# A decoder trunk on one core: the second attention map is added unscaled, weight sums work in half pieces, stores are issued later

## The chip, the cores and the metric

The program runs on one core of one Trainium2 chip. Its five engines work side by side, each from a queue of its own: TensorE (PE) multiplies matrices, VectorE (DVE) and ScalarE (ACT) work elementwise, GpSimd (POOL) does some elementwise work and here issues most stores, SyncE (SP) issues the loads. The metric is the device time of one execution in microseconds (us), as the median of three.

## The reference, cut to what matters

One layer over 2048 prompt tokens and eight single-token samples: pooling mixer and differential attention, cross-attention, a gated MLP, norms between. The change touches two parts. The differential attention of a head has two score maps:

```python
s = einsum('bqhcd,bkhcd->bhcqk', q, k) * 64 ** -0.5   # c = 0, 1
a = softmax(s + alibi_bias, causal)                   # each map on its own
w = a[:, :, 0] - lam * a[:, :, 1]
o = einsum('bhqk,bkhe->bqhe', w, v)
o = rmsnorm(o, subln_g, 1e-5) * (1 - lam_0)           # over the 128 channels of a head
```

The MLP multiplies the normed tokens by `w_up` (1024 x 5632) in float32.

## The kernel before

**Numbers.** Every product of the projections is made of three matmuls over a high and a low part of each operand, the high part by an ACT copy, the low part by a DVE subtraction (`split`, L93, and the weights' stages at L307 and L310).

**Stages.** Tokens go in four chunks of 512. Within the profiled span: the projections of chunks 0 and 1 (to about 300 us), the projections of chunks 2 and 3 woven with the attention of chunks 0 and 1 (to about 640 us), the attention of chunks 2 and 3 woven with output projection, norms and first cross-attention work (to about 1110 us), the rest of the cross-attention and the samples' attention (to about 1680 us), and the MLP (to the end).

**Attention.** A `Unit` (L1088) is 128 query rows of one head against up to 2048 keys, in halves of 1024 columns. PE makes the scores of both maps (L1111). DVE adds the position bias and finds the row's extreme (L1122), ACT takes the exponential in place with its row sum `l` (L1129). `combine` (L1133) makes `rc` = (1/l0, -lam/l1) on DVE (L1138, L1139), and POOL scales the second map T1 by rc[1] (L1141). `combine2` (L1143) on DVE makes T0 = T0 * rc[0] + T1 (L1146). PE turns T0 (`wT`, L1152), ACT copies it out (L1154), PE multiplies by V into `O` (L1163). After four units `att_post1` (L1186) norms `O` into `on`, and `att_post2` turns and stores it.

**Weight sums.** `sums_items` (L1510) builds, for each of 22 blocks of `w_up`, four sums and differences of quarter blocks that the MLP uses later: two loads of 512 KB on SP's queue (L1519), four DVE instructions of 128x512 (L1528 to L1532), two splits, four stores of 512 KB on POOL's queue (L1541) into `s_d`.

**Order.** The work is a list of items; `weave` spreads a second list through a first by each item's costs. `later` puts off a function until a clock, summed up from the costs of PE's items, has gone on by so much, and `due` runs what is due. Each engine then gets its instructions in an order that a scheduler of the framework sets, which can put rows of other units between two that the code issues together.

**Buffers.** Large tiles (1024 columns and more) share one ring of 41 buffers (`H`), smaller ones a ring of 6 (`St`); a new tile takes the buffer of the one 41 or 6 requests earlier, and waits until that is free, which for a stored tile is when its store has landed. SP and POOL issue in order.

Of the kernel before, what the change touches and what calls it, by code (L numbers as in the profile page):

```python
# [11 lines left out]
F32 = mybir.dt.float32  # L12
F32R = mybir.dt.float32r
# [35 lines left out]
def tile_trunk_step(ctx: ExitStack, tc: tile.TileContext, a, o):  # L49
# [12 lines left out]
    def H(name, dt=F32):  # L62
        return hp.tile([P, HT], dt, tag="H", name=name)

    def St(name, dt=F32):
        return sp.tile([P, SW], dt, tag="S", name=name)
# [4 lines left out]
    def Tn(name):  # L71
        return tp.tile([P, 8], F32, tag="t", name=name)
# [7 lines left out]
    def v3(t, k, n=None):  # L80
        n = n if n is not None else 1024 // k
        return t[:, : k * n].rearrange("p (k n) -> p k n", k=k)
# [4 lines left out]
    def f(ap):  # L87
        return ap.bitcast(F32)
# [267 lines left out]
    def item(specs, fn, cost=0.0, lat=0.0):  # L356


        return (specs, fn, cost, max(lat, cost, 0.3))
# [412 lines left out]
    def v_proj(vt, chunks):  # L772
        st = {}

        def fn(c, t2):
            def run(ws):
# [12 lines left out]
                if t2 == 2:  # L789
# [4 lines left out]
                    for hh in range(2):  # L794
# [3 lines left out]
                vv = St("vv")  # L798
                S.copy(vv[:, :512], ps)
                t0 = c * CH + 2 * t2 * P  # L800
                ST.dma_start(o["v_p"][0, 0, t0:t0 + 256, 2 * vt:2 * vt + 2, :].rearrange("(t p) h e -> p t (h e)", p=P),
                             v3(vv, 2, 256))
                j0 = (c % 2) * 4 + 2 * t2
                for hh in range(2):
                    ST.dma_start(v_d[c // 2][2 * vt + hh][:, j0:j0 + 2, :], v3(vv, 2, 256)[:, :, hh * P:(hh + 1) * P])
            return run

        specs = [cols256("w_in", 1536 + vt * 256, 0), cols256("w_in", 1536 + vt * 256, 1)]
# [255 lines left out]

    def att_load(h, nhf, old):
        def fn(_):
            K = [[None, None] for _ in range(2)]
            Vt = [None, None]
            for hf in range(nhf):
                for c in range(2):  # L1070
                    K[c][hf] = H("K", F32R)
                    SY.dma_start(f(K[c][hf][:, :1024]), k_d[hf][h][c])
                Vt[hf] = H("V")
                SY.dma_start(v3(Vt[hf], 8), v_d[hf][h])
            att[h, nhf] = (K, Vt)
        return fn
# [11 lines left out]
    class Unit:  # L1088
# [42 lines left out]
            return item([], fn, self.halves[hf][1] / 512 * 0.43)  # L1131

        def combine(self, _):  # L1133
            l, T1 = self.l, self.T[1]
            if len(self.halves) == 2:
                V.tensor_tensor(l[:, 0:2], l[:, 0:2], l[:, 2:4], ALU.add)
            self.rc = rc = Tn("rc")
            V.reciprocal(rc[:, 0:2], l[:, 0:2])  # L1138
            V.tensor_tensor(rc[:, 0:2], rc[:, 0:2], lamv, ALU.mult)  # L1139
            for hf, (k0, m) in enumerate(self.halves):  # L1140
                G.tensor_scalar(T1[hf][:, :m], T1[hf][:, :m], rc[:, 1:2], 1.0, ALU.mult, ALU.mult)  # L1141

        def combine2(self, _):  # L1143
            for hf, (k0, m) in enumerate(self.halves):
                T0, T1 = self.T[0][hf], self.T[1][hf]
                V.scalar_tensor_tensor(T0[:, :m], T0[:, :m], self.rc[:, 0:1], T1[:, :m], ALU.mult, ALU.add)  # L1146

        def turn(self, g):
            js = range(4 * g, min(4 * g + 4, self.i + 1))
# [36 lines left out]
    def att_post1(qc, h):  # L1186
        O = att["O", qc, h]
        sq = St("osq")
        S.activation(sq[:, :512], O, AF.Square)
        ss = Tn("oss")  # L1190
        V.tensor_reduce(ss[:, 0:4].rearrange("p (a o) -> p a o", o=1), v3(sq, 4, P), AX.X, ALU.add)
        r = rstd(ss[:, 0:4], P, 4, 1.0 / P, SUB_EPS)
        on = St("on")
        V.tensor_tensor(v3(on, 4, P), v3(O, 4, P), bc(r, [P, 4, P], 2), ALU.mult)
        att["on", qc, h] = on
# [314 lines left out]
    def sums_items(js):  # L1510


        st = {}

        def load(j):
            def fn(_):
                wa, wg = H("wa"), H("wg")
                for t, c0 in ((wa, j * P), (wg, DFF + j * P)):
                    SY.dma_start(v3(t, 8), a["w_up"][0, :, c0:c0 + P].rearrange("(k p) n -> p k n", p=P))  # L1519
                st[j] = wa, wg  # L1520
            return item([], fn, 0, 1.0)

        def add(j, i):
            def fn(_):
                wa, wg = st[j]
                a1, a2, g1, g2 = wa[:, :512], wa[:, 512:1024], wg[:, :512], wg[:, 512:1024]
                if i:
                    V.tensor_tensor(a1, g2, a1, ALU.subtract)  # L1528
                    V.tensor_tensor(a2, a2, a1, ALU.subtract)
                else:  # L1530
                    V.tensor_tensor(g2, g1, g2, ALU.add)
                    V.tensor_tensor(g1, a1, g1, ALU.subtract)  # L1532
            return item([], fn, 0, 1.0)

        def part(j, i):
            def fn(_):
                t = st[j][i]
                hi, lo = H("shi", F32R), H("slo", F32R)
                split(hi[:, :1024], lo[:, :1024], t[:, :1024])
                for z, p in enumerate((hi, lo)):  # L1540
                    ST.dma_start(s_d[j][:, i, z].rearrange("p s n -> p (s n)"), f(p[:, :1024]))  # L1541
            return item([], fn, 0, 1.0)

        out = []
        for j in js:
            out += [load(j), add(j, 0), add(j, 1), part(j, 1), part(j, 0)]
        return out

    def k4(t):
# [395 lines left out]
```

## Time and profile before

| | us |
|---|---|
| median of 3 runs (lowest, highest) | 3116.74 (3115.84, 3120.43) |
| the profiled execution's own time | 3116.27 |
| its span, first to last instruction | 3114.6 |
| PE busy in the span | 2939.9 (94%) |
| DVE busy | 2240.0 (72%) |
| ACT busy | 1351.9 (43%) |
| POOL busy | 516.2 (17%) |

The span is 1.7 us shorter than the execution's time. PE is busy for nearly all of it, and the share of PE is lowest in the first 100 us and between 300 and 1110 us. A wait is put down to the instruction whose end came last; the chain of waits follows the last instruction back to what released it, step by step.

### The profile page before, as it was taken

The page shows a single profiled execution, that of the slowest core. Times are in us where ns is not written, and L with a number is a line of the kernel's source. Part 1 is how long each engine was busy: PE and PEld are TensorE (multiplying, and loading weights), DVE is VectorE, ACT ScalarE, POOL GpSimd, SP SyncE. Part 2 cuts the span into 40 slices and gives each one's busy share as a digit, 9 for nine tenths or more (in the row PEclk, how much of TensorE's full clock was granted, in tenths as well). Part 3 has the DMA queues.
Part 4 walks back from the last instruction along what each step waited for, and adds up shares of the span by engine and source line. Part 5 has one row for each costly group of instructions (what it writes and reads, how often), then busy time and mean ns, then how long its engine had stood idle before and what let it go on. Part 6 is the DMA issues. An engine that isn't in the chain of part 4 may idle for free.

```text
span 3114.6 us, 52466 instructions
## 1 busy us (share of the span) xinstructions
PE 2939.9 (94%) x19806; PEld 2650.3 (85%) x19806; DVE 2240.0 (72%) x4032; ACT 1351.9 (43%) x2271; POOL 516.2 (17%) x961
## 2 busy tenths in 40 slices
PE   7999899889899898999989999999999999999998
PEld 6778789778788687689978899888899989999998
DVE  5734666467776668666778978888888777877777
ACT  5534445355665442334333344444444433443333
POOL 0244235312111115421000000010000010000000
PEclk9999999989999999999999999999999999999999
DMA  8777478835353357658759876687776786576762
GB/s 280 243 270 241 135 238 263 265 97 186 115 173 119 110 176 255 203 171 282 276 190 332 294 247 220 211 275 249 238 253 217 236 291 209 178 262 218 240 210 105
DMA packets 520511, 683.14 MB, mean 219 GB/s; under 512 B 27472, under 2 KB 342359, under 8 KB 520243
## 3 DMA queue, kind: packets, MB, share of 16 engines
q1 hardware_dynamic: 466525, 533.87, 52.8%
q0 software_dynamic: 39936, 135.17, 12.2%
q10 hardware_dynamic: 13798, 10.76, 1.1%
q8 instruction: 156, 2.56, 0.3%
q14 instruction: 96, 0.79, 0.1%
HBM read 549.12 MB, written 130.98 MB: 218 GB/s over the span
## 4 chain that ended last, share of the span: by engine, by line
PE 59%; DVE 8%; issue 4%; DMA 2%; ACT 2%; POOL 1%; DVEq 0%; ACTq 0%; POOLq 0%; SPq 0%
PE up L1613 15%; PE down L1729 15%; PE up L1615 7%; PE wo L483 3%; PE upB L1613 2%; PE S L99 2%; PE S L101 2%; PE S L100 2%; PE O L1163 2%; PE vo L99 1%; PE vo L100 1%; PE vo L101 1%; PE upB L1615 1%; PE sc L1111 1%; DVE T L1122 1%
## 5 line engine op out<-in xcount | busy, mean ns | idle before, releaser
L1729 PE MATMUL down<-act,whi 128*128 128x512 f32 (+1 forms) x1760 | 452.1, 351 | 3.2 <-ACT whi L307 3.1
L1613 PE MATMUL up<-xhi,shl 128*128 128x256 f32 (+1 forms) x2816 | 406.9, 285 | 7.9 <-DVE s L1618 6.3
L1613 PEld LDWEIGHTS up<-xhi,shl 128*128 128x128 f32 x2816 | 365.1, 188 | 37.9 <-DVE s L1618 13.2
L1667 ACT ACTIVATE cc<-Uf,vec 128x512 f32<-128x512 f32 (+1 forms) x176 | 143.9, 818 | 502.6 <-DVE Uf L1618 491.6
L310 DVE TENSOR_TENSOR wlo<-wraw,whi 128x1024 fp32r<-128x1024 f32 x256 | 310.2, 1220 | 38.5 <-ACT whi L307 30.2
L1729 PEld LDWEIGHTS down<-act,whi 128*128 128x128 f32 x1760 | 286.5, 189 | 36.6 <-ACT whi L307 3.5
L307 ACT CAST whi<-wraw 128x1024 fp32r<-128x1024 f32 x256 | 265.3, 1047 | 102.3 <-DMA wraw<-in_w_down_dram 29.3
L1729 PE MATMUL down<-act,wlo 128*128 128x512 f32 (+1 forms) x880 | 280.2, 350 | 0.1
L1672 POOL COPY halo<-Uf 128x2 f32<-128x2 f32 x176 | 56.7, 322 | 1275.5 <-DVE Uf L1618 1250.5
L1129 ACT ACTIVATE T<-T,mn 128x1024 f32<-128x1024 f32 (+4 forms) x192 | 171.9, 897 | 131.2 <-DVE mn L1122 120.5
L1615 PE MATMUL up<-xlo,shl 128*128 128x256 f32 (+1 forms) x1408 | 223.8, 281 | 0.0
L1111 PE MATMUL sc<-K,Q 128*128 128x512 f32 (+5 forms) x640 | 176.6, 394 | 37.8 <-DVE mn L1122 36.3
L1613 PE MATMUL up<-xhi,whl 128*128 128x256 f32 (+1 forms) x1408 | 199.3, 284 | 8.8 <-DVE whl L329 4.9
L1613 PEld LDWEIGHTS up<-xhi,whl 128*128 128x128 f32 x1408 | 183.9, 189 | 17.5 <-DVE whl L329 6.1
L1615 PEld LDWEIGHTS up<-xlo,shl 128*128 128x128 f32 x1408 | 191.3, 188 | 0.3
L1675 DVE SCALAR_TENSOR_TENSOR cc<-Uf,vec,cc 128x512 f32<-128x512 f32 x176 | 131.6, 748 | 73.6 <-ACT cc L1667 73.5
L329 DVE TENSOR_TENSOR whl<-wraw,whl 128x512 fp32r<-128x512 f32 x264 | 178.5, 683 | 0.4 <-ACT whl L327 0.4
L1733 DVE TENSOR_TENSOR xf<-xf,down 128x512 f32<-128x512 f32 (+1 forms) x240 | 134.9, 578 | 56.2 <-PE down L1729 55.0
L1729 PEld LDWEIGHTS down<-act,wlo 128*128 128x128 f32 x880 | 154.1, 188 | 22.5 <-DVE wlo L310 0.9
L1122 DVE CUSTOM_DVE_ANT_0 T<-sc,Dt 128x1024 f32<-128x1024 f32 (+7 forms) x128 | 125.8, 985 | 64.0 <-PE sc L1111 49.3
L1618 DVE TENSOR_TENSOR Uf<-up,s 128x256 f32<-128x256 f32 (+1 forms) x264 | 111.6, 423 | 83.0 <-PE up L1615 80.5
L327 ACT CAST whl<-wraw 128x512 fp32r<-128x512 f32 x264 | 155.2, 614 | 25.4 <-PE up L1615 6.4
(437 smaller groups left out, 7124.5 us busy)
## 6 DMA issues: line engine op xcount, KB each, us to landing
shl<-s_d SPq DMA_DIRECT2D x352, 512.0 KB
wraw<-in_w_up_dram SPq DMA_DIRECT2D x264, 256.0 KB
wraw<-in_w_down_dram SPq DMA_DIRECT2D x88, 512.0 KB
s_d<-shi POOLq DMA_DIRECT2D x44, 512.0 KB
s_d<-slo POOLq DMA_DIRECT2D x44, 512.0 KB
wraw<-in_w_in_dram SPq DMA_DIRECT2D x32, 512.0 KB
Q<-q_d SPq DMA_DIRECT2D x64, 256.0 KB
wraw<-in_w_out_dram SPq DMA_DIRECT2D x32, 512.0 KB
```

The source lines that it names most:

```text
L307: S.copy(self.hi[:, :1024], self.raw[:, :1024])
L310: V.tensor_tensor(self.lo[:, :1024], self.raw[:, :1024], f(self.hi[:, :1024]), ALU.subtract)
L327: S.copy(self.hl[:, :512], self.raw)
L329: V.tensor_tensor(self.hl[:, 512:1024], self.raw, f(self.hl[:, :512]), ALU.subtract)
L1111: PE.matmul(ps[:, j * 512:j * 512 + w], v3(Q[c], 2)[:, z, self.t * P:(self.t + 1) * P], K[c][hf][:, c0:c0 + w], start=z == 0, stop=z == 1)
L1122: V.tensor_tensor_reduce(out, pin, din, -SLOPE[self.h], 3.0e38 if hf == 0 else mn[:, 0:1], ALU.add, ALU.min, mn[:, hf:hf + 1])
L1129: S.activation(tg[:, :mg], tg[:, :mg], AF.Exp, bias=mn[:, last:last + 1], scale=-1.0, accum_out=self.l[:, 2 * g + c:2 * g + c + 1])
L1613: PE.matmul(out, wi[:, k, :], xh[:, k], start=k == 0 and wi is wl, stop=False)
L1615: PE.matmul(out, wh[:, k, :], xl[:, k], start=False, stop=k == 3)
L1667: S.activation(cc[:, :w], U[:, 2:2 + w], AF.Identity, bias=vc(CB + nt), scale=vc(CWT + 2 * FT + nt))
L1729: PE.matmul(out, st["w"][0][wi][:, p, n0:n0 + P], act[:, z + c0:z + c0 + n], start=st_ and p == 0, stop=en and p == g - 1)
L1733: V.tensor_tensor(xx[:, c0:c0 + n], xx[:, c0:c0 + n], out, ALU.add)
```

## The change

Four edits. **One:** T1 is no longer scaled by POOL. `combine` makes rc = (1/l0, 1/l1) and then rc[1] = l0 * (-lam) * (1/l1), and `combine2` makes T0 = T1 * rc[1] + T0, which is l0 times the old result. 1/l0 of the four units is kept in a tile `rcu` and comes in behind the values: `att_post1` multiplies the mean square twice by 1/l0 ahead of the root, and the root's reciprocal once. **Two:** the weight sums work on half pieces of a block, each in one buffer `ws`: four loads of 128 KB, four DVE instructions of 128x256, one split, two stores of 512 KB, each of them written in four runs of 256 columns per partition. The loads count 1.5, the other steps 0.5 each in the weave, 6 for a block where it was 5. **Three:** the sums' stores are an item behind the split. **Four:** the stores of V are put off by 2.6 on the clock (or until K and V are loaded), and the copy that the attention reads goes ahead of the output's.

```diff
@@ v_proj
-                ST.dma_start(o["v_p"]...)
                 j0 = (c % 2) * 4 + 2 * t2
-                for hh in range(2):
-                    ST.dma_start(v_d[c // 2][2 * vt + hh]...)
+                def store():
+                    for hh in range(2):
+                        ST.dma_start(v_d[c // 2][2 * vt + hh]...)
+                    ST.dma_start(o["v_p"]...)
+                later(2.6, store, "v")
@@ att_load
+            due("v")
@@ Unit.combine, combine2
-            self.rc = rc = Tn("rc")
-            V.reciprocal(rc[:, 0:2], l[:, 0:2])
-            V.tensor_tensor(rc[:, 0:2], rc[:, 0:2], lamv, ALU.mult)
-            for hf, (k0, m) in enumerate(self.halves):
-                G.tensor_scalar(T1[hf][:, :m], T1[hf][:, :m], rc[:, 1:2], 1.0, ALU.mult, ALU.mult)
+            if self.t == 0:
+                att["rc", self.qc, self.h] = tp.tile([P, 8], F32, tag="rcu", name="rcu", bufs=6)
+            rc = att["rc", self.qc, self.h][:, 2 * self.t:2 * self.t + 2]
+            self.rc = rc[:, 1:2]
+            V.reciprocal(rc, l[:, 0:2])
+            V.scalar_tensor_tensor(self.rc, l[:, 0:1], lamv[:, 1:2], self.rc, ALU.mult, ALU.mult)
...
-                V.scalar_tensor_tensor(T0[:, :m], T0[:, :m], self.rc[:, 0:1], T1[:, :m], ALU.mult, ALU.add)
+                V.scalar_tensor_tensor(T0[:, :m], T1[:, :m], self.rc, T0[:, :m], ALU.mult, ALU.add)
@@ att_post1
+        r0 = att["rc", qc, h][:, 0:8:2]
+        for _ in range(2):
+            V.tensor_tensor(ss[:, 0:4], ss[:, 0:4], r0, ALU.mult)
         r = rstd(ss[:, 0:4], P, 4, 1.0 / P, SUB_EPS)
+        V.tensor_tensor(r, r, r0, ALU.mult)
@@ sums_items
+        def load(j, q):
+                w = st[j, q] = H("ws")
+                for i, c0 in enumerate((j * P, DFF + j * P)):
+                    for h in range(2):
+                        r0 = h * 512 + q * 256
+                        SY.dma_start(v3(w[:, i * 512 + h * 256:i * 512 + (h + 1) * 256], 2, P),
+                                     a["w_up"][0, r0:r0 + 256, c0:c0 + P].rearrange("(k p) n -> p k n", p=P))
+            return item([], fn, 0, 1.5)
+        def add(j, q):
...
+                V.tensor_tensor(g2, g1, g2, ALU.add)        # and three more of 128x256
+        def part(j, q):
+                split(st["p"][0][:, :1024], st["p"][1][:, :1024], st.pop((j, q))[:, :1024])
+        def store(j, q):
+                for z, p in enumerate(st["p"]):
+                    ST.dma_start(s_d[j][:, :, z, :, q * 256:(q + 1) * 256], f(v3(p, 4)).rearrange("p (i s) n -> p i s n", i=2))
-            out += [load(j), add(j, 0), add(j, 1), part(j, 1), part(j, 0)]
+            for q in range(2):
+                out += [load(j, q), add(j, q), part(j, q), store(j, q)]
```

How this moves instructions is seen at three places. On DVE in the attention of chunks 2 and 3, where a unit with 1920 keys is combined beside the norm of the cross-attention's input (`h2lo`, `wlo` are splits), there stood before:

```order
L281 TENSOR_TENSOR h2lo<-x,h2hi 128x2x512
L1138 RECIPROCAL rc<-l 128x2
L1122 ISA T,mn<-sc,Dt 128x1024
L1122 ISA mn 128x1
L1139 TENSOR_TENSOR rc<-rc,lamv 128x2
L310 TENSOR_TENSOR wlo<-wraw,whi 128x1024 x2
L1146 SCALAR_TENSOR_TENSOR T<-T,rc 128x1024
L1146 SCALAR_TENSOR_TENSOR T<-T,rc 128x896
```

and near it in the change, where L1127 is the old L1122, L1146 and L1147 make the factors and L1152 is the combination:

```order
L1127 ISA T,mn<-sc,Dt,mn 128x128
L1127 ISA mn 128x1
L1146 RECIPROCAL rcu<-l 128x2
L1147 SCALAR_TENSOR_TENSOR rcu<-l,lamv,rcu 128x1
L1152 SCALAR_TENSOR_TENSOR T<-T,rcu 128x1024
L1127 ISA T,mn<-sc,Dt 128x1024
L1127 ISA mn 128x1
L310 TENSOR_TENSOR wlo<-wraw,whi 128x1024 x2
L1152 SCALAR_TENSOR_TENSOR T<-T,rcu 128x1024
```

The combination follows its factors at once; the splits that stood between them now stand behind its first half. On DVE at the end of four units (`oss` is the sum of squares, `rv` to `ry` the root), before:

```order
L187 TENSOR_SCALAR rv<-oss 128x4
L1528 TENSOR_TENSOR wa<-wg,wa 128x512
L190 TENSOR_TENSOR rt<-ry 128x4
L1529 TENSOR_TENSOR wa<-wa 128x512
L191 TENSOR_TENSOR rt<-rt,rv 128x4
L1122 ISA T,mn<-sc,Dt,mn 128x896
```

and at the same place in the change (L1200 is the new product with 1/l0, L1542 the last of the sums):

```order
L1197 TENSOR_REDUCE oss<-osq 128x4
L310 TENSOR_TENSOR wlo<-wraw,whi 128x1024 x2
L1200 TENSOR_TENSOR oss<-oss,rcu 128x4
L1141 TENSOR_TENSOR l<-l 128x2
L1542 TENSOR_TENSOR ws<-ws 128x256
L1200 TENSOR_TENSOR oss<-oss,rcu 128x4
L1146 RECIPROCAL rcu<-l 128x2
L187 TENSOR_SCALAR rv<-oss 128x4
L1147 SCALAR_TENSOR_TENSOR rcu<-l,lamv,rcu 128x1
L1152 SCALAR_TENSOR_TENSOR T<-T,rcu 128x1024
```

Two more small rows stand between the sum of squares and the root, with rows of other work between them. On POOL, where the projections of chunks 2 and 3 come to V, before:

```order
L1141 TENSOR_SCALAR T<-T,rc 128x1024
L1541 DMA s_d_156<-shi 128x1024
L1541 DMA s_d_156<-slo 128x1024
L801 DMA out_v_p_dram<-vv 128x2x256
L805 DMA v_d_0_140<-vv 128x2x128
L805 DMA v_d_1_141<-vv 128x2x128
L1541 DMA s_d_156<-shi 128x1024
L1541 DMA s_d_156<-slo 128x1024
L1141 TENSOR_SCALAR T<-T,rc 128x128
```

and in the change (L1554 are the sums' stores, L805 and L806 those of V):

```order
L1554 DMA s_d_156<-shi 256x2x256
L1554 DMA s_d_156<-slo 256x2x256
L755 COPY zsT<-kf 128x8
L744 DMA k_d_3_135<-kh 64x512 x2
L744 DMA k_d_3_135<-kl 64x512 x2
L751 DMA out_k_p_dram<-ks 128x4x128
L805 DMA v_d_0_140<-vv 128x2x128
L805 DMA v_d_1_141<-vv 128x2x128
L806 DMA out_v_p_dram<-vv 128x2x256
L1554 DMA s_d_156<-shi 256x2x256
```

POOL's queue holds stores and small copies alone there; the scalings are gone from between them.

## Rows read from the trace of the kernel before

**Rows 1.** The page: the span and the busy time of the engines.
```profile
span 3114.6 us, 52466 instructions
PE 2939.9 (94%) x19806; PEld 2650.3 (85%) x19806; DVE 2240.0 (72%) x4032; ACT 1351.9 (43%) x2271; POOL 516.2 (17%) x961
```

**Rows 2.** Stretches: length, PE, PEld, DVE, ACT, POOL busy; PE's clock, DMA, GB/s.
```profile
97.00:300.00 203.00, 197.86 (x1107) 169.25 (x1105) 113.33 (x165) 89.79 (x138) 76.19 (x135) 1.00 0.79 259
300.00:720.00 420.00, 381.37 (x2478) 342.62 (x2479) 259.68 (x545) 195.72 (x386) 131.50 (x205) 0.95 0.64 204
720.00:1110.00 390.00, 348.84 (x2342) 309.03 (x2341) 279.16 (x501) 228.74 (x441) 68.58 (x74) 0.97 0.42 137
1110.00:1684.00 574.00, 532.23 (x3354) 464.81 (x3353) 396.71 (x618) 215.27 (x346) 122.83 (x145) 0.97 0.69 232
1684.00:3114.00 1430.00, 1403.94 (x10047) 1297.47 (x10045) 1137.46 (x2103) 569.15 (x873) 107.40 (x355) 0.99 0.71 233
```

**Rows 3.** PE's waits from 300 to 1110 us: total us, times, longest us.
```profile
PE sc L1111 <- DVE mn L1122: 36.3, 20, 8.3
PE wT L1152 <- DVE T L1146: 13.6, 8, 4.1
```

**Rows 4.** DVE's waits from 300 to 720 us.
```profile
DVE T L1122 <- PE sc L1111: 50.5, 39, 5.4
DVE T L1146 <- POOL T L1141: 24.3, 24, 2.1
```

**Rows 5.** DVE's waits from 720 to 1110 us.
```profile
DVE T L1146 <- POOL T L1141: 21.4, 19, 1.9
DVE l L1136 <- ACT T L1129: 18.8, 10, 3.9
```

**Rows 6.** The chain of waits, 720 to 1110 us: shares of the stretch by line.
```profile
by line: PE O L1163 11.3%; PE sc L1111 8.9%; DVE T L1122 8.7%; PE wo L483 8.6%; issue 5.9%; PE wT L1152 5.9%; DVE T L1146 5.3%; POOL T L1141 3.6%; PE S L99 2.9%; PE S L101 2.9%; PE S L100 2.9%; ACT T L1129 2.6%; DVE wlo L310 2.5%; DMA Q<-q_
```

**Rows 7.** Pieces of that chain around 840 us: start us, us, what.
```profile
837.05 3.01 POOL T L1141
840.08 2.04 DVE T L1146
842.17 1.13 PE wT L1152 x4
```

**Rows 8.** Groups by shape, 300 to 1110 us: busy, mean ns | idle before.
```profile
L1146 DVE SCALAR_TENSOR_TENSOR T<-T,rc 128x1024 f32<-128x1024 f32 x40 | 63.5, 1594 | 31.1 <-POOL T L1141 31.1
...
L1139 DVE TENSOR_TENSOR rc<-rc,lamv 128x2 f32<-128x2 f32 x64 | 10.1, 158 | 1.2
...
L1141 POOL TENSOR_SCALAR T<-T,rc 128x1024 f32<-128x1024 f32 x40 | 51.2, 1283 | 242.6 <-DVE rc L1139 111.9 <-ACT T L1129 39.0 <-ACT wT L1154 35.4
```

**Rows 9.** DVE in order of time: a combination with no scaling beside it.
```profile
641.52 1.28 DVE L1146 SCALAR_TENSOR_TENSOR T<-T,rc 128x1024 f32<-128x1024 f32 x1
```

**Rows 10.** Groups by shape, the whole span: sums on DVE, stores on POOL.
```profile
L1618 DVE TENSOR_TENSOR Uf<-up,s 128x256 f32<-128x256 f32 x198 | 83.5, 421 | 59.6 <-PE up L1615 57.8
...
L1529 DVE TENSOR_TENSOR wa<-wa 128x512 f32<-128x512 f32 x22 | 15.1, 688 | 0.4
...
L1541 POOL DMA_DIRECT2D s_d<-shi x44 | 24.2, 551 | 214.0 <-ACT shi L94 202.6 <-PE z L483 5.8 <-ACT h2st L94 5.3
...
L751 POOL DMA_DIRECT2D out_k_p_dram<-ks x16 | 12.6, 787 | 8.4 <-ACT ks L750 3.6 <-issue 2.5 <-ACT om L1203 1.9
```

**Rows 11.** PE and SP in order of time around the longest stall.
```profile
591.85 0.74 PE L1111 MATMUL sc<-K,Q 128*128 128x448 f32 x1 [8.32 <-DVE mn L1122]
...
583.44 2.14 SPq L1519 DMA_DIRECT2D wa<-in_w_up_dram  x1
585.67 1.79 SPq L1519 DMA_DIRECT2D wg<-in_w_up_dram  x1
598.39 0.37 SPq L1519 DMA_DIRECT2D wa<-in_w_up_dram  x1
```

**Rows 12.** ACT's wait before that stall, 570 to 600 us.
```profile
ACT whi L307 <- DMA wraw<-in_w_out_dram: 9.1, 1, 9.1
```

## What was forecast from this

> **What bounds the kernel.** I read the page first: the span is 3114.6 us and PE is busy for 2939.9 us of it [rows 1], so all engines together can give back about 175 us, and only where PE stands idle. The stretches then say where that is [rows 2]. From 1684 us on, PE is busy for 1403.9 of 1430 us: the MLP is PE's own, and no edit adds or removes anything there. From 97 to 300 us it idles for 5.1 us. In the two stretches that hold the attention it idles for 38.6 us (300 to 720) and 41.2 us (720 to 1110), with a granted clock of 0.95 and 0.97 in the mean, and from 1110 to 1684 us for 41.8 us. Rows 11 show an idle piece of 8.3 us in one go. PE's waits name the releaser in the attention: mostly DVE, which has not yet emptied the banks of the scores (36.3 us) or not yet combined the maps (13.6 us) [rows 3]. DVE is not full there: it works for 259.7 of 420 us and 279.2 of 390 us [rows 2], so something holds it up. Its own waits name two things: PE's scores, which is the same ring of two banks seen from the other side, and the scaling on POOL, 24.3 us in the first stretch [rows 4] and 21.4 us in the second, where it is the longest wait of all [rows 5]. While DVE stands at L1146, every score that it should empty stands behind it in its queue, and PE waits for that. The chain of waits confirms that this is on the path: from 720 to 1110 us (390 us) it spends 3.6% in POOL's scaling and 5.3% in the combination behind it [rows 6]. One such place is seen whole: the scaling takes 3.01 us, the combination 2.04 us, then PE goes on with the turns [rows 7].
>
> **The change part by part.** The profiled execution took 3116.27 us, 1.7 us more than its span and 0.5 us under the median of 3116.74 us; I sum against 3116.3 us, and the difference is nothing here.
>
> The scaling goes. On the chain that is 3.6% of 390 us = 14.0 us less [rows 6]. DVE's small rows stay two for a unit, a reciprocal and a product. The combination keeps its size, but not its price: alone it took 1.28 us [rows 9], in the mean of 40 it took 1.594 us [rows 8], since its second half runs while POOL scales the other. 40 x 0.314 = 12.6 us of 63.5 us, a fifth. Of the 5.3% x 390 = 20.7 us on the chain [rows 6] a fifth is 4.1 us.
>
> The Trainium skill has a rule on this (SBUF — State Buffer, Who interferes with whom): a DVE instruction with two inputs in SBUF and a POOL instruction that reads SBUF share a read port, and whoever comes second waits for the whole of the other. If each of the 40 lost a whole scaling pass (1.283 us [rows 8]), 51 us of DVE time would come back, a third of it on the chain as for the combination itself, 17 us in place of 4.1 us. The mean of 1.594 us says that far less than the whole was lost, so the measured mean counts.
>
> From 300 to 720 us the chain cannot be read in this way, since its view does not reach back past 726 us. The bounds: nothing, if PE has other work at each such place, and 24.3 us if all that DVE waits there is PE's [rows 4]. DVE has slack in this stretch and PE's longest stall, 8.3 us, comes from a late load and not from POOL (ACT waited 9.1 us for it [rows 11, 12]). I take 4 us, nearer the lower end.
>
> The clock: in the stretch before 300 us, with 5.1 us of idle time, PE's granted clock is 1.00; where it idles for longer the mean is lower. 0.95 over 420 us and 0.97 over 390 us are 21.0 + 11.7 = 32.7 us of lost work, beside 79.8 us of idle time, 0.41 us for each [rows 2]. 22.1 us (14.0 + 4.1 + 4) less idle time would give 9 us by this ratio; since many of these stalls are short I take 4 us, with 0 and 9 as the bounds.
>
> The norm behind the values gets three more DVE rows of 128x4 in each of 16 groups. A row of 128x2 takes 158 ns [rows 8]: 48 x 0.158 = 7.6 us of DVE time, and half a us on the way from `oss` to `on`, with PE's turn of `on` behind it. The bounds are 0 (cover: the turn is put off by 6 on PE's clock) and 7.6 us. I take 2.5 us, a third, about DVE's part of the path.
>
> The weight sums: a block had four DVE rows of 0.688 us and gets eight of 128x256, which the nearest row of that shape puts at 0.421 us [rows 10]: 3.37 - 2.75 = 0.62 us more, 13.6 us over 22 blocks. Five blocks lie before 300 us, where PE hardly idles and loses nothing; 17 x 0.62 = 10.5 us fall in the rest. Bounds 0 and 10.5 us; I take 2.5 us. The splits stay as many and as large.
>
> Loads and stores: SP issues 8 loads for a block and not 2, so 132 more, at 0.37 us [rows 11] 49 us over some 1450 us of a queue that spends most of its time waiting for buffers. POOL's 88 stores of the sums go out in 512 runs each; the store of k with as many runs took 0.787 us to issue, against 0.551 us [rows 10], so 88 x 0.236 = 21 us more on POOL, against the scalings that leave it, 51.2 us for the 40 of 1024 columns alone [rows 8]; by the code (64 units, 32 of them with two halves) there are 56 smaller ones, estimated at half as much for each, some 36 us. POOL comes out ahead, and nothing that PE waits for is then left in its queue but the stores of q, k, V and the mix, which come earlier: V's stores no longer hold the queue until ACT has copied `vv`. Against that the small tiles of V are held for longer. Both signs are possible: -8 us (the stall of 8.3 us [rows 11] goes) to +10 us (one more like it, with its clock). I take 0.
>
> What is late next: behind the combination PE needs ACT's exponentials and the copies of `wT`; DVE already waits 18.8 us for ACT in the second stretch [rows 5], a second path close behind the first. I take 3 us back for it.
>
> Sum: -14.0 - 4.1 - 4 - 4 + 2.5 + 2.5 + 0 + 3 = -18.1 us, so 3098.2 us.
>
> **The rivals.**
> *More than that.* If DVE, no longer held, empties the scores early enough that PE's waits for it mostly go: 36.3 + 13.6 us [rows 3] less the 8.3 us of the late load leaves 41.6 us; three quarters of that and its clock at half the ratio is 31 + 6 = 37 us, 3079 us. For it: the released time on DVE (45.7 us of waits and 12.6 us of contention, less 7.6 and about 7 of additions within the attention) is as large as that. Against it: much of PE's wait for scores comes from DVE's own rows, splits for other units, that stay.
>
> *No change.* The wait changes its name: DVE gets to the scores earlier, but ACT's exponentials [rows 5] or PE's own order set the pace, and the additions eat the rest. Then the path keeps about 4 us of the gain, and that within the measurement: about 3113 us. Against it speaks that in rows 7 PE waits for precisely this pass, with ACT long done.
>
> *Slower.* The loads. SP issues in order, and the weights of the projections stand behind the pieces of the sums. Where its queue was crowded one load of the sums took 2.14 and 1.79 us to issue, not 0.37 [rows 11]; eight such take some 16 us where two took 4. PE's longest stall came when a weight of the output projection was late for ACT [rows 11, 12]. If three blocks out of the eight between 300 and 640 us each made such a stall, 3 x (8.3 + 3.4) = 35 us with the clock at 0.41, against the gain of 18: 3133 us. It decides from two such stalls on (23 us). For it speaks that this already happened once; against it that a block is spread over some 40 us, and weights are asked for several steps ahead.
> The Trainium skill speaks for this rival (DMA: Bandwidth & Descriptors, Rules for kernel authors): it wants many small transfers made into one large one. With its fitted cost of 2.0 us and the bytes at 436 GB/s (there for POOL's path, in Anatomy of one DMA), an estimate is 8 x 2.3 = 18.4 us for a block's loads one after the other against 2 x 3.2 = 6.4 us, 12 us more for each block if none overlapped. No row here shows that fixed part.
>
> **How the numbers follow.** 0.2%, about 6 us, is what a measurement of this kernel can tell from no change. The forecast, 8 to 30 us faster, has 0.48; more than that 0.17; no change 0.19; slower 0.16, with most of it under 3133 us. Faster by more than 6 us is then 0.65. The lower end of the range is the large case with a little of the store's stall, 3075 us; the upper end takes in half of the slower case, 3124 us. The forecast's own range is 3086 to 3108 us.
>
> **What would show it.** POOL's busy time falls by about 87 us for the scalings less 21 us for the stores, from 516 us to some 450 us. L1152 of the change at 1024 columns takes 1.28 us, and has no wait for POOL. PE's idle time from 720 to 1110 us falls from 41 us to about 25 us, and that stage ends earlier by 15 us or more; the waits of PE for the combination fall under 5 us. The stretch before 300 us and the MLP keep their lengths. The forecast is wrong if the idle time of PE in the attention stays and the chain goes through ACT's exponentials there, or if ACT's waits for weights grow past the 9.1 us of rows 12.

## The result and the profile after

The changed kernel takes 3087.36 us in the median of four runs (3079.39 to 3091.96), the kernel before 3118.59 us beside it: a ratio of 0.9894, with a 95% interval of 0.9871 to 0.9918. That is 33 us less (26 to 40 of 3118.59), where 18 us less had been forecast. The profiled execution of the changed kernel took 3084.29 us.

The page of the changed kernel, the lines that answer to [rows 1]:

```profile
span 3082.3 us, 52644 instructions
PE 2936.7 (95%) x19806; PEld 2650.9 (86%) x19806; DVE 2246.0 (73%) x4168; ACT 1355.8 (44%) x2271; POOL 458.2 (15%) x865
```

PE has the same number of matmuls and is idle for 145.6 us in place of 174.7 us (the span less its busy time): 29 of the 32 us by which the span is shorter are PE's idle time. POOL is busy for 58 us less.

Since stretches of fixed times no longer hold the same work, I cut both executions by PE's work: at its first `sc` matmul, the last `z`, the first `wo`, the last `O` and the first `up`. Four stretches lie between these (bounds of a stretch, its length, then the columns of [rows 2]): projections of chunks 2 and 3 with the first attention; the end of that attention; the attention of chunks 2 and 3; the rest of the cross-attention. First the kernel before:

```profile
298.50:529.00 230.50, 211.27 (x1369) 190.27 (x1368) 151.05 (x325) 108.63 (x218) 79.10 (x134) 0.96 0.67 212
529.00:647.60 118.60, 98.57 (x707) 90.69 (x706) 63.51 (x140) 53.11 (x104) 39.66 (x57) 0.88 0.70 228
647.60:1123.30 475.70, 434.54 (x2839) 382.91 (x2838) 329.48 (x587) 267.80 (x513) 81.63 (x89) 0.97 0.43 141
1123.30:1614.70 491.40, 457.48 (x2791) 397.60 (x2790) 347.06 (x538) 181.24 (x291) 117.85 (x124) 0.97 0.66 221
```

and the same four of the changed kernel:

```profile
293.60:512.00 218.40, 208.51 (x1370) 188.46 (x1368) 158.61 (x366) 112.00 (x221) 68.15 (x113) 0.98 0.69 221
512.00:625.40 113.40, 97.64 (x707) 90.01 (x706) 64.45 (x157) 51.81 (x103) 32.37 (x45) 0.89 0.78 241
625.40:1084.80 459.40, 434.47 (x2838) 386.51 (x2836) 322.23 (x621) 268.89 (x513) 19.61 (x26) 0.97 0.46 147
1084.80:1581.10 496.30, 459.48 (x2790) 398.67 (x2789) 350.43 (x565) 181.65 (x291) 128.10 (x124) 0.96 0.66 219
```

The gain is spread: 4.9 us before the first score (298.5 to 293.6 us), 12.1, 5.2 and 16.3 us in the three stretches of the attention, and 4.9 us are given back in the fourth. What lies behind them, mostly the MLP, takes 1.3 us more. In the third stretch PE works as long as before (434.5 us) and idles for 24.9 us in place of 41.2.

PE's waits from 294 to 1085 us, which answer to [rows 3], and DVE's from 625 to 1085 us, which answer to [rows 5]:

```profile
PE sc L1116 <- DVE mn L1127: 29.2, 17, 6.8
...
PE wT L1158 <- DVE T L1152: 1.4, 1, 1.4
```
```profile
DVE T L1127 <- PE sc L1116: 42.0, 32, 4.0
DVE l L1141 <- ACT T L1134: 21.5, 11, 3.5
```

PE's wait for the combination is down from 13.6 to 1.4 us, that for emptied score banks from 36.3 to 29.2 us. DVE's waits for POOL are gone, its waits for the exponentials are still there. The chain of waits from 700 to 1085 us, which answers to [rows 6]:

```profile
by line: PE O L1169 17.1%; PE sc L1116 14.8%; PE wo L483 11.8%; PE wT L1158 7.7%; DVE T L1127 5.2%; DVE T L1152 3.3%; ACT T L1134 3.3%; PE S L99 2.7%; PE S L101 2.7%; PE S L100 2.7%; issue 2.3%; PE memkv L99 1.8%; PE memkv L100 1.8%; PE mem
```

POOL's scaling (14.0 us there before) is no longer on it, and the combination has 3.3% of 385 us, 12.7 us against 20.7 us. More of the chain is now PE's own (`O` from 11.3 to 17.1%).

### The profile page after: what moved, and what is told of

It is laid out like the page before. It is cut to its first block, busy times and chain, and to the rows that moved or that the text cites. A ratio compares the mean times of both kernels' runs of the same rounds, so it can differ in the third digit from the quotient of the medians.

```text
span 3082.3 us, 52644 instructions
## 1 busy us (share of the span) xinstructions
PE 2936.7 (95%) x19806; PEld 2650.9 (86%) x19806; DVE 2246.0 (73%) x4168; ACT 1355.8 (44%) x2271; POOL 458.2 (15%) x865
## 4 chain that ended last, share of the span: by engine, by line
PE 81%; DVE 8%; issue 4%; DMA 3%; ACT 3%; POOL 1%; ACTq 0%; DVEq 0%; SPq 0%; POOLq 0%
PE up L1627 16%; PE down L1743 15%; PE up L1629 7%; PE z L483 7%; PE wo L483 4%; PE O L1169 4%; PE sc L1116 4%; PE upB L1627 2%; PE S L99 2%; PE S L100 2%; PE S L101 2%; PE vo L99 2%; PE vo L100 2%; PE vo L101 2%; PE wT L1158 2%
## 5 line engine op out<-in xcount | busy, mean ns | idle before, releaser
L1116 PE MATMUL sc<-K,Q 128*128 128x512 f32 (+5 forms) x640 | 176.6, 393 | 32.6 <-DVE mn L1127 29.2
L1127 DVE CUSTOM_DVE_ANT_0 T<-sc,Dt 128x1024 f32<-128x1024 f32 (+7 forms) x128 | 126.3, 988 | 69.9 <-PE sc L1116 66.2
```

The source lines that it names most:

```text
L1116: PE.matmul(ps[:, j * 512:j * 512 + w], v3(Q[c], 2)[:, z, self.t * P:(self.t + 1) * P], K[c][hf][:, c0:c0 + w], start=z == 0, stop=z == 1)
```

## The experiments

Each ratio is that of the experiment to the kernel before, run beside it, with a 95% interval in brackets; 0.001 is 3.1 us.

**The parts alone.** The change was taken apart by its edits: the attention and the norm behind it (edit 1), the weight sums in half pieces (edit 2), their stores in an item of their own (edit 3), the V stores put off (edit 4).

Edit 1 alone:

```diff
-            for hf, (k0, m) in enumerate(self.halves):
-                G.tensor_scalar(T1[hf][:, :m], T1[hf][:, :m], rc[:, 1:2], 1.0, ALU.mult, ALU.mult)
...
-                V.scalar_tensor_tensor(T0[:, :m], T0[:, :m], self.rc[:, 0:1], T1[:, :m], ALU.mult, ALU.add)
+                V.scalar_tensor_tensor(T0[:, :m], T1[:, :m], self.rc, T0[:, :m], ALU.mult, ALU.add)
```

> The kernel before with edit one alone (the second map unscaled, 1/l0 behind the values). Theory A, the scaling pass on POOL and what it holds up on DVE is nearly the whole gain: 0.8 to 1.1% faster (25 to 35 us), with both attention stages shorter by 14 us or more each. Rival B, the first attention stage (its 331 us, 17 us shorter in the change) gains from the stores and the weight sums, not from the scaling: 0.4 to 0.6% faster (12 to 20 us), the first stage shorter by under 6 us.

Measured: 3098.57 us, ratio 0.9922 (0.9903 to 0.9942), 24 us less. That is just under theory A's range, and theory A fails on one of its two stages: the attention of chunks 2 and 3 is 18.0 us shorter, but that of chunks 0 and 1 only 6.7 us and not 14.

Edits 2 and 3 alone:

```diff
-            out += [load(j), add(j, 0), add(j, 1), part(j, 1), part(j, 0)]
+            for q in range(2):
+                out += [load(j, q), add(j, q), part(j, q), store(j, q)]
```

> The kernel before with edits two and three alone (weight sums in half pieces, their stores an item later). Theory A: within 0.3% of before, on either side, since it adds 0.6 us of DVE time for a block and takes nothing off. Rival B: 0.3 to 0.5% faster (10 to 15 us), through shorter waits for buffers in the first attention stage.

Measured: 3096.67 us, ratio 0.9931 (0.9908 to 0.9953), 21.5 us less, more than either theory had.

Edit 4 alone, `later(2.6, store, "v")` around the V stores:

> The kernel before with edit four alone (stores of V put off). Theory A: within 0.2% of before. Rival B: 0.1 to 0.3% faster, since POOL's queue is no longer held until V is copied and the scaling of the units behind it starts earlier; then the gain lies between 530 and 640 us.

Measured: 3120.51 us, ratio 0.9995 (0.9982 to 1.0009): nothing that can be measured.

Edits 1 and 4 together:

> The change without edits two and three (weight sums as before). Theory A: as fast as the whole change or a little faster, 1.0 to 1.3% under before, since the stage behind the attention no longer loses the 5 us that it lost in the change. Rival B: 0.5 to 0.8% under before, the sums' share missing.

Measured: 3099.44 us, ratio 0.993 (0.9911 to 0.995). So the scaling is not nearly the whole gain: the sums alone bring almost as much, and the two do not add up (24 + 21.5 us against 33). Beside the attention edit the sums are worth some 9 to 11 us.

**Which part of the sums.** Edit 3 alone:

```diff
                 split(hi[:, :1024], lo[:, :1024], t[:, :1024])
-                for z, p in enumerate((hi, lo)):
-                    ST.dma_start(s_d[j][:, i, z].rearrange("p s n -> p (s n)"), f(p[:, :1024]))
-            return item([], fn, 0, 1.0)
+                st["p"] = hi, lo
+            return item([], fn, 0, 0.5)
+        def store(j, i):
...
```

> Edit 3 alone: whole blocks of weight sums as before, the two stores of a half in an item behind the split. Theory C (the sums gain through POOL's queue: an s_d store at its head waits for ACT's shi, up to 11.5 us, and holds the mix_d store behind it, on which DVE's plo and PE's pool matmul wait, 8 us in four PE stalls before 400 us): most of the 21.5 us of edits 2 and 3 together comes from here, -12 to -20 us, ratio 0.994 to 0.996, and the four stalls of the pool matmul fall to under 2 us in all. Rival D (half pieces: 8 small loads and one buffer of the ring in place of two, shorter rows on DVE): the later store alone is worth under 5 us, ratio 0.9985 to 1.0015, and the stalls stay.

Measured: 3125.48 us, ratio 1.0007 (0.9993 to 1.0021). Edit 2 alone, with the two stores of a piece in the item of its split:

> Edit 2 alone: half pieces, but each piece's two stores issued in the same item as its split. Theory C: with the stores still right behind the split, POOL's head waits for ACT as before; under 7 us of gain, ratio 0.998 to 1.001. Rival D: most of the 21.5 us of edits 2 and 3, -14 to -22 us, ratio 0.993 to 0.9955.

Measured: 3103.89 us, ratio 0.9935 (0.9919 to 0.9951), 20 us less. Theory C falls: the later store does nothing that can be measured, the half pieces bring about all. Cut by PE's work as above, half pieces gain 3.2 us before the first score, 9.3, 4.3 and 9.9 us in the three stretches of the attention, and lose 4.8 us in the fourth.

The observation behind theory C was real. In the kernel before POOL issues in order, and a store of the mix stands behind two stores of the sums and a scaling (first fence, POOL). Its buffer of the ring of 6 comes free late, DVE's `plo` waits 2.88 us for it, and PE 2.61 us for `plo` (second fence, DVE, and third, PE):

```profile
347.37 0.56 POOL L1541 DMA_DIRECT2D s_d<-shi  x1 [2.94 <-ACT shi L94]
347.96 1.14 POOL L1141 TENSOR_SCALAR T<-T,rc 128x768 f32<-128x768 f32 x1
349.07 0.59 POOL L1541 DMA_DIRECT2D s_d<-slo  x1
349.66 0.55 POOL L719 DMA_DIRECT2D mix_d<-pm  x1
```
```profile
358.85 0.69 DVE L95 TENSOR_TENSOR plo<-pr,phi 128x512 fp32r<-128x512 f32 x1 [2.88 <-DMA mix_d<-pm]
```
```profile
359.60 0.50 PE L99 MATMUL pool<-plo,pws 128*128 128x512 f32 x1 [2.61 <-DVE plo L95]
```

PE's waits for `plo` from 60 to 420 us, in the kernel before, with the later store alone, with half pieces alone, and in the run below with both pieces loaded together:

```profile
PE pool L99 <- DVE plo L95: 8.6, 5, 2.6
```
```profile
PE pool L99 <- DVE plo L95: 8.3, 5, 2.6
```
```profile
PE pool L99 <- DVE plo L95: 0.9, 1, 0.9
```
```profile
PE pool L99 <- DVE plo L95: 3.5, 3, 2.2
```

The half pieces take these stalls away, the later store does not. How they do it is not shown. POOL's order at this place is the same with half pieces alone, a store of the mix behind two stores of the sums and a scaling, and `plo` waits for nothing there:

```profile
342.76 0.91 POOL L1141 TENSOR_SCALAR T<-T,rc 128x768 f32<-128x768 f32 x1
343.63 0.98 POOL L1540 DMA_DIRECT2D s_d<-slo  x1
344.60 0.58 POOL L719 DMA_DIRECT2D mix_d<-pm  x1
```
```profile
351.26 0.69 DVE L95 TENSOR_TENSOR plo<-pr,phi 128x512 fp32r<-128x512 f32 x1
```

From the end of the store's issue to `plo` it is 6.1 us here and 8.6 us in the kernel before, so the buffer came free sooner behind an issue that stood where it had stood. POOL's order alone is therefore not the cause.

**What it is in half pieces.** The run with half pieces alone, but both pieces loaded in one item, sums and splits by pieces:

```diff
-            for q in range(2):
-                out += [load(j, q), add(j, q), part(j, q)]
+            out += [item([], lambda _, j=j: [load(j, q)(_) for q in range(2)], 0, 1.5)]
+            for q in range(2):
+                out += [add(j, q), part(j, q)]
```

> Half pieces without the later store, but both pieces of a block are loaded in one item, so that two of the ring's buffers are taken at once as by a whole block. Theory F (DVE's runs of sums work: a whole block puts four sums of 0.69 us ahead of its first split and two splits of 1.2 us near each other, and in the kernel before a split of the pooling branch at 150.69 us stood 4.5 us behind its input, with half pieces 2.1 us): the gain of half pieces stays, -14 to -22 us, ratio 0.993 to 0.9955. Rival G (a piece takes one buffer of the ring where a block took two, so other loads start sooner): the gain goes, ratio 0.998 to 1.001. Rival L (eight loads of 128 KB in place of two of 512 KB): the gain stays here too.

Measured: 3118.62 us, ratio 0.9982 (0.9972 to 0.9992). The same with the sums of both pieces in a row, `[add(j, 0), add(j, 1), part(j, 0), part(j, 1)]`:

> As the run of half pieces loaded together, but the sums of both pieces come in a row and then the two splits, as in a whole block: loads of 128 KB, eight sums of 0.42 us, two splits. Theory F: the gain goes for the most part, ratio 0.9975 to 1.001. Rival L: it stays, ratio 0.993 to 0.9955. Rival G: no gain, as in the other run.

Measured: 3116.11 us, ratio 0.9976 (0.9965 to 0.9988). Both keep 6 to 8 us of the 20. Theory F (shorter runs of sums work) falls, since the first of the two has the short runs; rival L falls, since both have eight loads of 128 KB. Left is what rival G names: the second piece is loaded, and takes its buffer, at a step of its own. The runs don't tell apart its place in the ring of 41, its place in SP's queue, and the spacing of the items, which changes too: a block is six items that count 6 with half pieces alone, and five that count 4.5 in these two.

What it does to the attention can be seen. The stretch of the attention of chunks 2 and 3 is 465.8 us long with half pieces alone and 477.3 us when they are loaded together (475.7 before). Around the stall of [rows 7], DVE in the run with the pieces loaded together, then with half pieces alone:

```profile
829.97 2.35 DVE L310 TENSOR_TENSOR wlo<-wraw,whi 128x1024 fp32r<-128x1024 f32 x2
833.26 3.09 DVE L1146 SCALAR_TENSOR_TENSOR T<-T,rc 128x1024 f32<-128x1024 f32 x2 [0.94 <-POOL T L1141]
```
```profile
818.62 2.04 DVE L1146 SCALAR_TENSOR_TENSOR T<-T,rc 128x1024 f32<-128x1024 f32 x1 [1.31 <-POOL T L1141]
820.58 1.21 DVE L95 TENSOR_TENSOR slo<-ws,shi 128x1024 fp32r<-128x1024 f32 x1
821.71 2.35 DVE L310 TENSOR_TENSOR wlo<-wraw,whi 128x1024 fp32r<-128x1024 f32 x2
```

and the turn on PE that waits for it, in the same order:

```profile
835.34 0.48 PE L1152 MATMUL wT<-ident,T 128*128 128x128 f32 x1 [4.11 <-DVE T L1146]
```
```profile
820.71 0.55 PE L1152 MATMUL wT<-ident,T 128*128 128x128 f32 x3 [1.43 <-DVE T L1146]
```

The first is the kernel before again, where this wait is 4.11 us too: two splits of a weight stand between the factor and the combination, on DVE's queue and beside POOL's pass. With half pieces alone the scheduler has put the first combination ahead of them. So part of what the sums gain here is POOL's pass again, moved out of its company and not removed. Over the stretch PE's waits for the combination are 6.5 us with half pieces alone, 11.2 us with the pieces loaded together, and 10.2 us before. That fits the gains that don't add in this stretch: 18.0 us for the attention edit alone (457.7 us long), 9.9 us for half pieces alone, 16.3 us for the whole change. What the sums add to the whole change lies ahead of this stretch, by these single profiles: 10.6 of the 17.3 us in the two stretches before it, and most of the 4.9 us before the first score.

**The hop and its company.** On the whole change, the POOL pass was put back between the factor and the combination:

```diff
+            for hf, (k0, m) in enumerate(self.halves):
+                T1 = self.T[1][hf]
+                G.tensor_scalar(T1[:, :m], T1[:, :m], self.rc, 1.0, ALU.mult, ALU.mult)
...
-                V.scalar_tensor_tensor(T0[:, :m], T1[:, :m], self.rc, T0[:, :m], ALU.mult, ALU.add)
+                V.scalar_tensor_tensor(T0[:, :m], T1[:, :m], 1.0, T0[:, :m], ALU.mult, ALU.add)
```

> The whole change, but a POOL pass over the second map (times the same factor, in place) stands again between the factor and DVE's combination, whose scalar is then 1.0: the hop, its contention and POOL's 80 passes are back, everything else of the change stays. Theory A (the hop is what the attention edit removes): back by what attention is worth in this company, about 10 to 20 us, 3097 to 3107 us, ratio 0.993 to 0.996, and DVE's combination waits for POOL over 40 us in chunks 2 and 3. Rival (the gain of the attention edit is in DVE's own instructions and their order): within 4 us of the whole change.

Measured: 3109.16 us, ratio 0.9958 (0.9942 to 0.9974). Next, a POOL pass of nearly that size for which no combination waits:

```diff
+                G.tensor_scalar(junkp[:, :min(m, 768)], self.T[1][hf][:, :min(m, 768)], self.rc, 1.0, ALU.mult, ALU.mult)
```

> The whole change, and beside it a POOL pass that reads the second map (up to 768 columns of it) once the factor is there and writes a tile that nobody reads: POOL's passes and their contention with DVE are back, DVE's combination doesn't wait for them; the next writer of the map's buffer does. Theory A as predicted (14 us of the scaling's cost is the hop, 4 us the contention): 2 to 6 us above the whole change, 3089 to 3095 us, ratio 0.990 to 0.992. Rival (the engines' contention, not the hop, makes up the 19 us that the hop cost when it was put back): 12 to 19 us, ratio 0.9935 to 0.996.

Measured: 3092.82 us, ratio 0.9908 (0.9893 to 0.9923). The pass on the path costs 0.0064, 20 us, the pass beside it 0.0014, 4 us. The two intervals do not overlap, so a pass on the path costs more than one beside it; that of the latter overlaps the whole change's, so that the company may cost nothing. By the medians some four fifths are the hop, a share that the intervals don't fix. DVE's waits for POOL are back in the first of the two, from 633 to 1105 us, though below the 40 us expected:

```profile
DVE T L1155 <- POOL T L1150: 22.8, 21, 1.6
```

The combination of 1024 columns in the attention of chunks 2 and 3, in the whole change, with the pass beside it, and with the hop:

```profile
L1152 DVE SCALAR_TENSOR_TENSOR T<-T,rcu 128x1024 f32<-128x1024 f32 x35 | 44.9, 1284 | 0.9
```
```profile
L1155 DVE SCALAR_TENSOR_TENSOR T<-T,rcu 128x1024 f32<-128x1024 f32 x35 | 46.1, 1319 | 0.9
```
```profile
L1155 DVE SCALAR_TENSOR_TENSOR T<-T 128x1024 f32<-128x1024 f32 x35 | 52.3, 1502 | 20.8 <-POOL T L1150 20.5
```

These are first halves. With the pass beside, the company falls on the second halves, here those of 896 columns in the whole change and with the pass beside:

```profile
L1152 DVE SCALAR_TENSOR_TENSOR T<-T,rcu 128x896 f32<-128x896 f32 x4 | 4.6, 1145 | 0.0
```
```profile
L1155 DVE SCALAR_TENSOR_TENSOR T<-T,rcu 128x896 f32<-128x896 f32 x4 | 7.2, 1796 | 0.0
```

All 62 combinations of the stretch keep DVE busy for 64.2 us in the whole change, 75.8 us with the pass beside and 76.0 us in the kernel before. So the run with the pass beside brings back about all the DVE time that the company costs, and loses 4 us or less by it: the price lies in the wait more than in DVE's time.

At the places read singly, the engine that begins second pays. In the kernel before, POOL's pass over the second half begins just ahead of the combination of the first:

```profile
1104.47 2.21 POOL L1141 TENSOR_SCALAR T<-T,rc 128x1024 f32<-128x1024 f32 x2 [0.77 <-PE wT L1152]
```
```profile
1105.61 2.14 DVE L1146 SCALAR_TENSOR_TENSOR T<-T,rc 128x1024 f32<-128x1024 f32 x1 [1.32 <-POOL T L1141]
```

The first pass, with DVE waiting, takes 1.1 us; beside the second, DVE takes 2.14 us in place of 1.28 us [rows 9]. In the run with the pass beside, DVE begins first, at 805.87 us, and POOL takes 1.90 us for 768 columns, where eight such passes take 1.063 us in the mean in the kernel before:

```profile
806.03 1.90 POOL L1150 TENSOR_SCALAR junkp<-T,rcu 128x768 f32<-128x768 f32 x1 [8.75 <-DVE rcu L1148]
```

**Two more.** Edits 1 to 3, the V stores as before:

> Edits 1 to 3, the V stores as before. If the V stores are worth nothing in company either (alone 0.9995): within 3 us of the whole change, 3084 to 3091 us, ratio about 0.9895. Rival: attention (-24 alone) and sums (-21.5 alone) add up to -45 and the V stores in company take 12 of it back: about 3075 us, ratio 0.9855.

Measured: 3092.67 us, ratio 0.9895 (0.9878 to 0.9913), that of the whole change. The whole change with sums and splits in quarters:

```diff
-                out += [load(j, q), add(j, q), part(j, q), store(j, q)]
+                out += [load(j, q), add(j, q, 0), part(j, q, 0), add(j, q, 1), part(j, q, 1), store(j, q)]
```

> The whole change, but sums and splits in quarter pieces (loads and stores in halves): sixteen sums of 128x128 and four splits of 128x512 a block. Theory F: the longest run of sums work falls again, from 1.7 to about 1.2 us, against about 0.9 us more DVE time a block over 16 blocks (14 us, mostly beside PE): 0 to -6 us against the whole change, ratio 0.9875 to 0.9895. Rival (the run's length no longer decides, the extra DVE time does): 3 to 10 us slower than the whole change, ratio 0.9905 to 0.9925.

Measured: 3092.15 us, ratio 0.9892 (0.9878 to 0.9906), no difference from the whole change that can be measured. Theory F's range, which takes in no gain, holds it too, so the run does not show that shorter runs of sums work help; the added DVE time costs nothing that can be seen. No run measurably beat the whole change.

## Why the prediction was right, and where it was wrong

*The sign and the size.* Faster was right. 33 us is more than the forecast's 18 us. The time lies inside the outer bounds and 1.4 us inside the lower end of the forecast's own range; by the ratio the gain is beyond its 8 to 30 us, in what the rival "more than that" had. The terms of the attention edit came to 20.6 us (the sum without the sums' 2.5 us) and measured 24 us; the sums, entered as a loss, brought the rest. That the range held with the sign of one term wrong is owed to its width, and is luck as far as the sums go. The rival's own way to such a gain, PE's waits for emptied scores mostly going, did not happen: they fell from 36.3 to 29.2 us.

*The scaling off the chain (14.0 us) and the combination's price (4.1 us).* Right in mechanism and about right in size. The third stretch lost 16.3 us, 18.0 us with the attention edit alone. The combination takes 1.284 us, as forecast, and waits for next to nothing (0.9 us in 35). PE's idle time from 720 to 1110 us was forecast at about 25 us and is 24.3 us. That the hop counts for more than its company, 14 to 4, fits the two runs with a POOL pass, 20 us with both and 4 us for the company alone. But the two are not apart in the chain as the prediction took them: the 3.01 us of the scaling in [rows 7] began 0.26 us behind two splits on DVE and are mostly company, since the same pass takes 1.1 us with DVE waiting.

On the rule of the Trainium skill that the later of the two engines waits for the whole of the other (SBUF — State Buffer, Who interferes with whom): the prediction took the mean of 1.594 us against it, and read it wrongly. The pass beside a combination of 1024 columns is that of the second half, which is narrower in most units, and some combinations have none beside them, as in [rows 9]; the mean is made of both. Where one is beside it, DVE loses most of it: 0.86 us of 1.1 us at 1105.61 us. This agrees with the rule, and so does POOL's 1.90 us behind DVE in the run with the pass beside. The price of 4.1 us came from the mean itself and does not hang on this.

*The stretch from 300 to 720 us (4 us).* For the attention edit about right: alone it took 6.4 and 0.3 us from the first two of the four stretches. Of the changed kernel's 17.3 us there, the other 10.6 us come with the sums.

*The weight sums (+2.5 us).* This is the step that failed. It priced the instructions. On DVE they came as forecast: a row of 128x256 takes 0.42 us, and DVE is busy for 6 us more in all. A store takes 0.91 us to issue on POOL (0.79 had been taken). The groups that answer to [rows 10]:

```profile
L1540 DVE TENSOR_TENSOR ws<-ws 128x256 f32<-128x256 f32 x44 | 18.6, 424 | 1.0
...
L1554 POOL DMA_DIRECT2D s_d<-shi x44 | 40.1, 911 | 240.4 <-ACT shi L94 201.6 <-ACT whi L307 37.6 <-issue 1.1
```

Alone the half pieces gain 20 us (15 to 25). The dearer stores are 32 us more on POOL and not 21, and POOL is busy for 458 us in place of the forecast's 450. The forecast treated a block as an amount of work and not as something that sits among other work: the runs show that the step at which the second piece is loaded decides, and that stalls go and DVE's rows change places with it; by which buffer or queue is not shown. Five blocks before 300 us were costed at nothing, "where PE hardly idles"; but of PE's 8.6 us of waits for `plo` up to 420 us about half lie before 300 us, and 0.9 us were left with half pieces. The first 298.5 us, which were to keep their length, are 4.9 us shorter. The rows of waits given ahead of the prediction begin at 300 us, so that they left these out.

*Loads and stores (0, between -8 and +10 us).* The V stores are worth nothing that can be measured, alone and in company. What the half pieces bring lies outside the lower bound: the bound went by the one stall of 8.3 us, and the gain is spread over the stretches. The slower rival's crowding came about on SP, where twelve loads in a row took 13.96 us:

```profile
566.60 13.96 SPq L1531 DMA_DIRECT2D ws<-in_w_up_dram  x12
```

They added no stall of PE: in the second of the four stretches PE waits for emptied banks five times before and after, 15.7 and 15.2 us. The stall of [rows 11] answers to one of 5.93 us in the changed kernel, and ACT's wait for the weight ahead of it, as in [rows 12], is down from 9.1 to 7.4 us; SP had asked for that weight at 564.47 us, ahead of the twelve loads:

```profile
573.43 2.08 PE L1116 MATMUL sc<-K,Q 128*128 128x512 f32 x4 [5.93 <-DVE mn L1127]
```
```profile
ACT whi L307 <- DMA wraw<-in_w_out_dram: 7.4, 1, 7.4
```

The longest is now the stall behind it, which was the second longest before. DVE goes through the norm of four units and three splits of the mix ahead of its release (605.23 to 611.97 us), not through the sums. The kernel before, then the changed one:

```profile
633.72 0.69 PE L1111 MATMUL sc<-K,Q 128*128 128x128 f32 x2 [5.08 <-DVE mn L1122]
```
```profile
612.37 0.69 PE L1116 MATMUL sc<-K,Q 128*128 128x128 f32 x2 [6.83 <-DVE mn L1127]
```

The Trainium skill's advice to make many small transfers into one (DMA: Bandwidth & Descriptors, Rules for kernel authors) had spoken for this rival; measured, half pieces with eight loads of 128 KB in two steps are 0.65% faster than whole blocks with two of 512 KB, and in one step 0.2%, so here the size of the loads did no harm that can be seen, and the step at which they are asked for counts.

*The norm (+2.5 us) and what is late next (+3 us).* The three rows take about 161 ns each, against 158 ns forecast; no run has them alone. DVE's waits for the exponentials did not grow: 21.5 us in the third stretch, against 23.1 us there before. No run shows the 3 us.

*The clock (4 us).* Over the three stretches of the attention, length times what the clock lacks to 1.00 is 37.7 us before and 30.6 us after: about 7 us won, and about 5 lost again in the fourth. The clock is read to two digits, which leaves either sum open by some 4 us, so the 4 us of the forecast fit and are not shown.

## What to carry to other kernels

A pass on another engine between two dependent instructions costs by its place on the path and by what stands behind the waiting instruction, not by its busy time: take it from the chain of waits, and split hop from contention before you price it. A group's mean hides which of two engines began first, and so who pays: look at single places. Work that nobody waits for still sets the order of everything around it: when it is cut into pieces or moved, read the waits of the whole span for stalls that come from shared buffers and in-order queues, and give its price both signs. Before you say that a stall grew or shrank, find the same work in both traces: the longest stall after need not be the longest before. Two edits that relieve the same stall don't add up.

## What was not expected of the hardware

The stretch of the cross-attention, which no edit touches but for some sums blocks, changes its length from kernel to kernel, and in part with PE's granted clock. Edits 1 to 3, then the half pieces with the sums in a row:

```profile
1087.50:1592.80 505.30, 464.79 (x2790) 401.20 (x2789) 350.73 (x565) 181.00 (x291) 127.71 (x124) 0.95 0.66 215
```
```profile
1119.70:1606.30 486.60, 456.40 (x2791) 396.48 (x2790) 349.17 (x562) 181.16 (x291) 123.89 (x124) 0.98 0.67 224
```

Length times granted clock is 480.0 us for the first and 476.9 us for the second, 476.7 for the kernel before and 476.4 for the changed one, so nearly constant within the two digits of the clock. But the 18.7 us between the two above are 8.4 us of PE's busy time and 10.3 us of its idle time, and its waits for named releasers are 33.6 us in the first and 29.4 us in the second. From the kernel before to the changed one PE is busy for 2.0 us more and idle for 2.9 us more in this stretch. So the clock explains a part of the loss there; what in the order of PE's work lowers it for longer stays open.
